# Mixture-of-experts stage: scatter woven with the next gather behind the whole down product, and a weight ring of one slab more

## The chip, the cores and the metric

One core of one Trainium2 chip. The time is the device time of one execution in microseconds (us), and of several executions the median counts. Matmuls run on TensorE (PE; its weight loads are listed as PEld), elementwise work on VectorE (DVE), ScalarE (ACT) and GpSimd (POOL). SyncE (SP) issues the transfers from memory in one queue, in its program's order; sixteen DMA engines carry them out.

## The reference, cut to what matters

One layer over 512 tokens of 1024 channels, all in float32. A token mixer (a state-space branch and a Fourier branch) fills the first part of the kernel and isn't touched. The second part is a routed feed-forward layer with 16 experts, where each expert picks its 64 best tokens:

```
aff = softmax(h @ w_router);  top_aff, top_idx = top_k(aff.T, 64)
xe  = h[top_idx]                                   # gather, 16 experts x 64 tokens
hid = silu(xe @ w_e_gate) * (xe @ w_e_up)          # 1024 -> 1024 each
ye  = (hid @ w_e_down) * top_aff                   # 1024 -> 1024
out = zeros.at[top_idx].add(ye)                    # scatter
x   = x + g2 * rms_norm(out, w)
```

The weights of the experts are 16 x 3 x 4 MB, about 201 MB, each byte read once.

## The kernel before, in words

The experts run two at a time, in eight pairs (the loop `for q in range(NE // 2)`, L1116). The two experts of a pair have 64 tokens each and take the two column halves of the TensorE array, so that their matmuls run side by side. Per pair:

- DVE compares the tokens' slot numbers with a row of counters (L1121), which gives a 0/1 matrix `pm_` of 512 tokens by 128 slots.
- The gather multiplies `h2` with `pm_` (L1129): eight channel tiles `kt`, four token chunks each. ACT moves each tile into `xe` and applies the modulation (L1131). After every two tiles the gate product `pg` uses them (`expert_mm`, L1082, with `ks=(k,)`), so gather and gate product alternate in four rounds.
- `pm_` is transposed into `pT` (L1135), and each slot's affinity `afs` is computed (L1139). Then comes the up product `pu` (L1082 again).
- ACT applies silu (L1150), DVE multiplies by `pu` (L1151), TensorE transposes `hid` (L1154), and ACT moves the transposes out (L1155).
- The down product `pd` (L1167) runs in four column blocks `m` of 256. After each block `scatter` (L1089) forms a high part `yeh` on ACT (L1093) and the rest `yel` on DVE (L1094), multiplies both with `pT` (L1100, eight matmuls of 256 columns) and adds them to the accumulators `acc` on DVE (L1105). In the last pair it also squares the sums (L1111, L1113) and multiplies them by the gate row on POOL (L1114).

At the end comes the norm (L1173 to L1175) and the output (L1183, L1184).

The weights come as slabs of 1 MB (128 partitions x 2048 floats): eight each for gate, up and down per pair, 24 in all, two (one per expert) for each quarter `k` of a product. `ring_tile` (L1051) places slab after slab in slots of on-chip memory, first in the order of `FIRST`, then round `RING` (15 slots). A slab's transfer is issued when TensorE has read the slot's earlier content for the last time; SP issues in the slabs' order and waits at the first that isn't free. The first 19 entries of `FIRST` are different slots.

```python
    FIRST = (21, 22, 23, 8, 10, 11, 12, 13, 14, 16, 0, 3, 9, 4, 6, 5, 1, 2, 20, 21, 22, 8, 23)
    RING = (10, 11, 12, 13, 14, 16, 0, 3, 4, 1, 2, 20, 21, 22, 23)
```

Slots 7 and 8 hold `xe` and `pm_` of alternating pairs, slot 9 holds `hid` and its transposes, slots 5 and 6 `acc`. On-chip result banks (PSUM) come from two pools: five for products (`MM`), three for small things (`SD`: gather, transposes, scatter).

The order of instructions on each engine is set by the framework's scheduler, from the order in which they are traced and from its own estimate of when inputs are ready; it may move an instruction past others. `in_order` pins the traced order where it is called; in the expert stage it isn't.

Of the kernel before, what the change touches and what calls it, by code (L numbers as in the profile page):

```python
# [9 lines left out]
F32 = mybir.dt.float32  # L10
# [21 lines left out]
# columns of the per-partition constants  # L32
# [26 lines left out]
def block_kernel(ctx: ExitStack, tc: tile.TileContext, a: dict, out: bass.AP):  # L59
# [62 lines left out]
    # ---------------------------------------------------------------- x, norms  # L122
# [24 lines left out]
    # triangular and other masks  # L147
# [17 lines left out]
    # sel[32 g + i, i] = 1: sums the partial products of the column tiles  # L165
# [5 lines left out]
    # the table of Silu, which has the functions of the first steps too  # L171
# [11 lines left out]
    def rstd_tok(y, ssum, m, t, n):  # L183
        """y = 1/sqrt(ssum/n + eps)"""
# [30 lines left out]
    def bcast_rows(dst, src, n):  # L215
        """dst[:, 128 c + t] = src[t, c] on all partitions"""
# [7 lines left out]
    def sum_squares(pss, src, slots, w):  # L224
        """sums over the channels, token-major"""
# [40 lines left out]
    def warm(dst, n):  # L266
        """keeps the tensor engine's clock up over a wait"""
# [62 lines left out]
    # ---------------------------------------------------------------- in-projection  # L330
# [5 lines left out]
    def conv(psum, ct, dst, rows, width):  # L336
        """centred depthwise convolution of a channel tile, then SiLU"""
# [14 lines left out]
    def wtile(idx, slot=None):  # L352
        """hi and lo parts of unit idx of the streamed weights"""
# [18 lines left out]
    # first group: contraction tiles in the outer loop, as their modulation becomes known  # L372
# [41 lines left out]
    # dt of both directions, token-major: chunks 0..3 of x, then 0..1 of ctx  # L414
# [6 lines left out]
    # the products with the hi and with the lo part on partitions 0.. and 48.., added up when they are transposed  # L421
# [7 lines left out]
    with tc.high_priority():  # L429
# [6 lines left out]
        # softplus(raw + bias) = max(v, 0) + 2 atanh(u / (2 + u)), u = exp(-|v|)  # L436
# [49 lines left out]
        # context: weights of the final states, [chunk, (dir, head)]  # L486
# [11 lines left out]
        # running sums as rows, through memory, to be read back on all partitions  # L498
# [7 lines left out]
    # ---------------------------------------------------------------- bidirectional SSD of a group  # L506
# [4 lines left out]
    def ssd(g):  # L511
# [40 lines left out]
        # C.B of every chunk, [s, t]  # L552
# [6 lines left out]
        # skip term  # L559
# [79 lines left out]
    # remaining modulation rows: products with silu(c) along the free dimension  # L639
# [14 lines left out]
    # the recurrences interleaved with the projections that they leave the tensor engine to  # L654
# [10 lines left out]
    def weave(pattern, main, fill):  # L665
        """steps of both in the pattern's order, then what is left of them"""
# [12 lines left out]
    # ---------------------------------------------------------------- Fourier branch  # L679
# [43 lines left out]
    # ---------------------------------------------------------------- merge of the branches  # L723
# [37 lines left out]
    # router with the second norm's gain folded in, and the logits of its shift  # L761
# [36 lines left out]
    def mix_step(dst, w, c, kt):  # L798
        """adds the contribution of contraction tile kt to one half of the output projection of a token chunk"""
# [6 lines left out]
    # the order of the units in the stream: 12 of w_ssd_out with one of the first half of w_out after every third  # L806
# [33 lines left out]
    # ---------------------------------------------------------------- output projection, residual, second norm  # L840
# [5 lines left out]
    # affinities, the chunks c as [c % 2, c / 2]  # L846
# [5 lines left out]
    # sums of squares over the channels: [step, (mixer output of the step's chunk, residual of the chunk before), half]  # L852
# [5 lines left out]
    def half(c, n, p):  # L858
        """mean square and product with the gate row, for one half of the columns"""
# [9 lines left out]
    def rsqrt(step, lo, hi, between=()):  # L869
        """rsd = 1/sqrt(mean square + eps) of the step's columns lo..hi"""  # L870
# [29 lines left out]
    def logits(c):  # L900
        """by expert, the contraction over four column tiles; then summed and token-major"""
# [36 lines left out]
    # affinities by expert: those of the first half of the tokens on partitions 0.., of the second on 32..  # L938
# [65 lines left out]
    # ---------------------------------------------------------------- routing: top CAP tokens of every expert  # L1004
# [4 lines left out]
    # the CAP-th of both sorted halves together: i of one and CAP - i of the other  # L1009
# [5 lines left out]
    # on all partitions; tokens above it, and those equal to it in order, fill the slots  # L1015
# [10 lines left out]
    # running counts of both kinds; every token above the value comes before those equal to it  # L1026
# [16 lines left out]
    # ---------------------------------------------------------------- experts, two at a time  # L1043
    acc = None
    wnames = ("w_eg", "w_eu", "w_ed")

    FIRST = (21, 22, 23, 8, 10, 11, 12, 13, 14, 16, 0, 3, 9, 4, 6, 5, 1, 2, 20, 21, 22, 8, 23)
    RING = (10, 11, 12, 13, 14, 16, 0, 3, 4, 1, 2, 20, 21, 22, 23)
# [7 lines left out]
    def weights(kind, q):  # L1056
        """slabs of the two experts, alternating"""
        tiles = {}
        for k in range(4):
            if kind == "w_eu" and q == NE // 2 - 1 and k == 2:  # L1060
                G3.append(ring_tile("g3")[:, 0:1024])
                for n in range(2):
                    p = SD(f"g3{n}")
                    bcast_rows(p, mod2[:, 24 + 4 * n:28 + 4 * n], 4)
                    act.copy(G3[0][:, 512 * n:512 * n + 512], p)
            for e in range(2):
                tiles[k, e] = ring_tile(f"{kind}{q}{k}{e}")
            cuts = CUTS[k] if kind == "w_ed" and q == NE // 2 - 1 else (0, 2048)
# [5 lines left out]
    G3 = []  # L1074

    def expert_mm(w, lhs, pout, ks=(0, 1, 2, 3)):
        for k in ks:
            for i in range(2):
                kt = 2 * k + i
                for n in range(2):  # L1080
                    for e in range(2):
                        pe.matmul(pout[n][64 * e:64 * e + 64, :], lhsT=lhs(kt)[:, 64 * e:64 * e + 64],  # L1082
                                  rhs=w[k, e][:, 1024 * i + 512 * n:1024 * i + 512 * n + 512],
                                  start=(kt == 0), stop=(kt == KT - 1))
# [4 lines left out]
    def scatter(q, m, pd, pT, afs):  # L1089
        """adds the experts' outputs in a block of 256 columns to their tokens; after the last pair their squares and gate"""  # L1090
        yeh = tp.tile([P, 256], F32, name=f"yeh{q}{m}", tag="sz")
        yel = tp.tile([P, 256], F32, name=f"yel{q}{m}", tag="xw")
        act.activation(R(yeh), pd, AF.Copy, scale=afs)  # L1093
        dve.scalar_tensor_tensor(R(yel), pd, afs, yeh, op0=ALU.mult, op1=ALU.subtract)  # L1094
        for i in range(2):
            p = SD(f"sc{q}{m}{i}")
            pv = v(p, 0, 2, 256)
            for c in range(2):
                for k, y in enumerate((yeh, yel)):
                    pe.matmul(pv[:, c], lhsT=R(pT[:, 2 * i + c]), rhs=R(y), start=(k == 0), stop=(k == 1))  # L1100
            av = v(acc[i], 0, 2, 1024)[:, :, 256 * m:256 * m + 256]
            if q == 0:
                dve.tensor_copy(av, pv)
            else:
                dve.tensor_add(av, av, pv)  # L1105
            if q == NE // 2 - 1:
                for c in range(2):
# [8 lines left out]
    for q in range(NE // 2):  # L1116
# [17 lines left out]
        for c in range(NCH):  # L1134
            pe.transpose(p[:, 128 * c:128 * c + 128], pm_[:, c], ident)  # L1135
# [130 lines left out]
```

## Time and profile before

| | |
|---|---|
| runs, median (lowest to highest) | 1171.88 us (1169.7 to 1176.0), 3 runs |
| profiled execution, span of its instructions | 1169.3 us (no other time of it is given) |
| TensorE busy | 1118.4 us, 96% of the span |
| DVE, ACT, POOL busy | 45%, 37%, 8% |
| memory traffic | 289.70 MB, 248 GB/s over the span |
| gate, up, down products: busy | 126.6, 118.1, 120.9 us |
| gather, scatter products: busy | 67.7, 34.1 + 31.1 us |

Busy time of TensorE is a union of matmuls whose ends are modelled, so how densely they run is read from the distance of their starts, not from this share. The expert stage runs from about 651 us to the end; `PEclk` is the granted clock of TensorE, 1.00 for 2.4 GHz and 0.50 for 1.2 GHz.

### The profile page before, as it was taken

How to read it: one execution, taken by the hardware profiler on the slowest of the kernel's cores; microseconds unless marked ns; L12 is line 12 of the kernel's file. 1: busy time of each engine (PE TensorE's matmuls, PEld its weight loads, DVE VectorE, ACT ScalarE, POOL GpSimd, SP SyncE). 2: the span in 40 equal slices, each digit the busy share in tenths (PEclk: the TensorE clock that was granted, in tenths of full speed). 3: DMA queues.
4: the chain of work that ended last, by engine and by line, in shares of the span. 5: the costliest groups of instructions: out<-in, count | busy, mean ns of one | idle time of the engine just before them, and what ended most of it. 6: DMA issues, size and time to landing. Idle time of an engine off the chain costs nothing. (4 is left out here: it accounts for less than half of the span.)

```text
span 1169.3 us, 16246 instructions
## 1 busy us (share of the span) xinstructions
PE 1118.4 (96%) x6596; PEld 766.3 (66%) x6596; DVE 529.0 (45%) x917; ACT 431.3 (37%) x688; POOL 96.7 (8%) x118
## 2 busy tenths in 40 slices
PE   8999999999899999999999999999999999999994
PEld 4788868778688887887886545454545454554542
DVE  5677988686686668744346211111102030201115
ACT  4357886877774532423236111111111111110112
POOL 1002132211121100001011000000000000000004
PEclk9999999999999999999999999999999999999997
DMA  8613243322424388733386698999999999999951
GB/s 313 232 44 94 89 111 89 111 76 88 135 84 153 151 301 303 257 121 100 103 338 263 244 363 323 392 419 420 417 384 420 374 419 372 420 370 420 358 170 73
DMA packets 57019, 289.70 MB, mean 248 GB/s; under 512 B 6928, under 2 KB 15600, under 8 KB 29936
## 3 DMA queue, kind: packets, MB, share of 16 engines
q1 hardware_dynamic: 56944, 288.66, 65.3%
q8 instruction: 52, 0.85, 0.3%
q14 instruction: 23, 0.19, 0.0%
HBM read 286.43 MB, written 2.21 MB: 247 GB/s over the span
## 5 line engine op out<-in xcount | busy, mean ns | idle before, releaser
L1151 DVE TENSOR_TENSOR hid<-hid,pu 128x512 f32<-128x512 f32 x16 | 11.0, 688 | 297.2 <-PE pu L1082 297.2
L1082 PE MATMUL pg<-w_eg,pk 128*64 128x512 f32 x512 | 126.6, 599 | 0.0
L1167 PE MATMUL pd<-w_ed,hid 128*64 128x256 f32 x1024 | 120.9, 382 | 0.0
L1082 PE MATMUL pu<-w_eu,pk 128*64 128x512 f32 x512 | 118.1, 593 | 0.0
L272 ACT CAST whl<-raw 128x1024 fp32r<-128x1024 f32 x71 | 74.4, 1050 | 113.4 <-PE gt L334 41.0
L273 DVE TENSOR_TENSOR whl<-raw,whl 128x1024 fp32r<-128x1024 f32 x71 | 90.6, 1279 | 46.0 <-ACT whl L272 45.7
L1167 PEld LDWEIGHTS pd<-w_ed,hid 128*64 128x64 f32 x1024 | 72.8, 137 | 38.2 <-ACT hid L1155 1.2
L1082 PEld LDWEIGHTS pu<-w_eu,pk 128*64 128x64 f32 x512 | 42.7, 136 | 66.5 <-issue 65.8
L1131 ACT ACTIVATE pk<-xe,mod 128x128 f32<-128x128 f32 x64 | 29.3, 457 | 140.4 <-PE xe L1129 140.4
L1082 PEld LDWEIGHTS pg<-w_eg,pk 128*64 128x64 f32 x512 | 36.6, 136 | 61.0 <-issue 56.9
L1129 PEld LDWEIGHTS xe<-pk,h 128*128 128x128 f32 x512 | 60.7, 191 | 21.3 <-issue 20.1
L1129 PE MATMUL xe<-pk,h 128*128 128x128 f32 x512 | 67.7, 281 | 0.2 <-DVE pk L1121 0.2
L1093 ACT ACTIVATE yeh<-pd,afs 128x256 fp32r<-128x256 f32 x32 | 15.1, 473 | 136.4 <-PE pd L1167 136.4
L1094 DVE SCALAR_TENSOR_TENSOR yel<-pd,afs,yeh 128x256 fp32r<-128x256 f32 x32 | 15.5, 484 | 105.1 <-ACT yeh L1093 105.1
L1114 POOL TENSOR_TENSOR acc<-acc,g 128x512 f32<-128x512 f32 x8 | 10.3, 1302 | 516.3 <-ACT jk L1113 515.9
L334 PE MATMUL gt<-hhi,whl 128*128 128x512 f32 x128 | 50.2, 392 | 0.0
L332 PE MATMUL gt<-hhi,whl 128*128 128x512 f32 x128 | 50.0, 391 | 0.0
L333 PE MATMUL gt<-hlo,whl 128*128 128x512 f32 x128 | 49.8, 389 | 0.0
L573 DVE TENSOR_TENSOR rm<-rm,misc 128x768 f32<-128x768 f32 x32 | 31.8, 995 | 39.0 <-POOL rm L571 38.9
L332 PE MATMUL pj<-hhi,whl 128*128 128x512 f32 x120 | 48.5, 404 | 0.0
L334 PE MATMUL pj<-hhi,whl 128*128 128x512 f32 x120 | 48.2, 401 | 0.0
L333 PE MATMUL pj<-hlo,whl 128*128 128x512 f32 x120 | 48.0, 400 | 0.0
(408 smaller groups left out, 2352.0 us busy)
## 6 DMA issues: line engine op xcount, KB each, us to landing
w_eg<-in_w_eg_dram SPq DMA_DIRECT2D x64, 1024.0 KB, 9.8
w_eu<-in_w_eu_dram SPq DMA_DIRECT2D x64, 1024.0 KB, 10.9
w_ed<-in_w_ed_dram SPq DMA_DIRECT2D x56, 1024.0 KB, 7.7
raw<-in_w_rest_dram SPq DMA_DIRECT2D x71, 512.0 KB, 3.4
wm<-in_wmod_dram SPq DMA_DIRECT2D x16, 1024.0 KB, 6.8
rm<-rowd SPq DMA_DIRECT2D x32, 384.0 KB, 5.6
wmod<-in_wmod_dram SPq DMA_DIRECT2D x8, 1024.0 KB, 7.8
w_ed<-in_w_ed_dram SPq DMA_DIRECT2D x12, 512.0 KB, 6.7
```

The source lines that it names most:

```text
L272: act.copy(hi, src)
L273: dve.tensor_sub(lo, src, hi.bitcast(F32))
L332: pe.matmul(dst, lhsT=wh, rhs=hi, start=(kt == 0 and start), stop=False)
L333: pe.matmul(dst, lhsT=wh, rhs=lo, start=False, stop=False)
L334: pe.matmul(dst, lhsT=wl, rhs=hi, start=False, stop=(kt == nk - 1 and stop))
L573: dve.tensor_tensor(mk, mk, csm[:, :, c, hs:hs + 3][:, :, :, None].to_broadcast([P, 2, 3, 128]), op=ALU.add)
L1082: pe.matmul(pout[n][64 * e:64 * e + 64, :], lhsT=lhs(kt)[:, 64 * e:64 * e + 64], rhs=w[k, e][:, 1024 * i + 512 * n:1024 * i + 512 * n + 51 ...
L1093: act.activation(R(yeh), pd, AF.Copy, scale=afs)
L1094: dve.scalar_tensor_tensor(R(yel), pd, afs, yeh, op0=ALU.mult, op1=ALU.subtract)
L1129: pe.matmul(p[:, 0:128], lhsT=tv(h2, c)[:, 128 * kt:128 * kt + 128], rhs=pm_[:, c], start=(c == 0), stop=(c == NCH - 1))
L1131: act.activation(xe[:, kt], p[:, 0:128], AF.Identity, bias=SH2[:, kt:kt + 1], scale=G2[:, kt:kt + 1])
L1167: pe.matmul(pd[-1][64 * e:64 * e + 64, o:o + 256], lhsT=hidT[:, kt, 64 * e:64 * e + 64], rhs=wd[m, e][:, 256 * kt:256 * kt + 256], start=( ...
```

## The change

Everything ahead of the experts stays (comments there are dropped). In the expert stage:

- `gather(q)` is a function of its own that yields after each of its eight channel tiles. Four tiles share one small bank and are moved out together. Pair 0's gather runs whole before the loop; the gather of pair `q + 1` runs at the end of pair `q`, tile by tile in turn with the eight steps of `scatter(q)` (two column halves of 512 by four token chunks, two matmuls of 512 columns each).
- The gate product is one run of 64 matmul instructions without gathers between, as the up product was. The affinities, the transposes of `hid` and those of `pm_` follow the up product in this order.
- The down product of all four blocks runs ahead of the scatter. `scaled` writes high and low parts of 512 columns into slot 8 (`ys`). Only in the last pair they are formed per block of 256, and block `m - 1` is scattered behind block `m` of the product (`scatter_last`).
- `xe` and `pm_` use slot 7 alone; `hid`, its transposes and `pT` move to small buffers. `RING` gets slot 9 and has 16 slots. The last pair's gate row `G3` is made between its gate and up products.
- `hold_order` pins the traced order of the whole stage on TensorE, and on no other engine.

```diff
+    FIRST = (21, 22, 23, 8, 10, 11, 12, 13, 14, 16, 0, 3, 9, 4, 6, 5, 1, 2, 20, 21, 22, 23, 10, 11)
+    RING = (12, 13, 14, 16, 0, 3, 9, 4, 1, 2, 20, 21, 22, 23, 10, 11)
...
+    def gather(q):
+        pk_ = S(f"pk{q}", 7)
+        xe, pm_ = v(pk_, 0, 8, 128), v(pk_, 1024, 4, 128)
+        dve.tensor_tensor(pm_.rearrange("p c (e s) -> p c e s", e=2), iota[:, None, None, :].to_broadcast([P, 4, 2, 64]),
+                          slot[:, :, 2 * q:2 * q + 2][:, :, :, None].to_broadcast([P, 4, 2, 64]), op=ALU.is_equal)
+        picked[q] = (xe, pm_)
+        for kt in range(KT):
+            if kt % 4 == 0:
+                p = v(SD(f"xe{q}{kt}"), 0, 4, 128)
+            for c in range(NCH):
+                pe.matmul(p[:, kt % 4], lhsT=tv(h2, c)[:, 128 * kt:128 * kt + 128], rhs=pm_[:, c], start=(c == 0),
+                          stop=(c == NCH - 1))
+            if kt % 4 == 3:
+                for k in range(kt - 3, kt + 1):
+                    act.activation(xe[:, k], p[:, k % 4], AF.Identity, bias=SH2[:, k:k + 1], scale=G2[:, k:k + 1])
+            yield
+
+    def scatter(q, ys, pT):
+        for n in range(2):
+            for c in range(NCH):
+                p = SD(f"sc{q}{n}{c}")
+                for k in range(2):
+                    o = 1024 * k + 512 * n
+                    pe.matmul(p, lhsT=R(pT[c // 2][:, 128 * (c % 2):128 * (c % 2) + 128]), rhs=R(ys[:, o:o + 512]),
+                              start=(k == 0), stop=(k == 1))
+                av = tv(acc, c)[:, 512 * n:512 * n + 512]
+                if q == 0:
+                    dve.tensor_copy(av, p)
+                else:
+                    dve.tensor_add(av, av, p)
+                yield
...
+    def scaled(ys, lo, hi, pd, afs):
+        yh_, yl_ = ys[:, lo:hi], ys[:, 1024 + lo:1024 + hi]
+        act.activation(R(yh_), pd, AF.Copy, scale=afs)
+        dve.scalar_tensor_tensor(R(yl_), pd, afs, yh_, op0=ALU.mult, op1=ALU.subtract)
...
+    run(gather(0))
+    for q in range(NP):
+        last = q == NP - 1
+        xe, pm_ = picked.pop(q)
+        wg = weights("w_eg", q)
+        expert_mm(wg, xe, pg)
...
+        expert_mm(wu, xe, pu)
...
+            if last:
+                scaled(ys, 256 * m, 256 * m + 256, pd[:, o:o + 256], afs)
+                if m > 0:
+                    scatter_last(m - 1, ys, pT)
+            elif m % 2 == 1:
+                scaled(ys, 256 * m - 256, 256 * m + 256, pd, afs)
+        if last:
+            scatter_last(3, ys, pT)
+        else:
+            weave("fsfsfsfsfsfsfsfs", scatter(q, ys, pT), gather(q + 1))
+    hold_order(begin_experts, {pe.engine})
```

In `weave`, `f` takes a step of the gather and `s` a step of the scatter.

## Rows read from the trace of the kernel before

**Rows 1.** Busy time of the engines in stretches of one pair; columns in the first line.

```profile
core 0: us, PE busy (x) PEld busy (x) DVE busy (x) ACT busy (x) POOL busy (x), PEclk, DMA share, GB/s
653.38:713.81 60.43, 58.94 (x374) 31.71 (x373) 9.68 (x16) 9.98 (x20) 0.00 (x0) 1.00 0.84 329
962.96:1026.36 63.40, 61.08 (x374) 33.26 (x376) 9.05 (x15) 8.81 (x19) 0.00 (x0) 1.00 0.97 398
```

**Rows 2.** Chain that ended last, one pair: start us, us, engine, output, count.

```profile
966.54 1.98 PE xe L1129 x16
...
981.52 0.59 PE pT L1135 x4
982.11 0.80 PE as L1139 x8
...
986.48 13.75 PE pu L1082 x61
1000.33 0.70 DVE hid L1151
1001.07 0.65 PE ht L1154 x4
1001.72 3.65 PE pd L1167 x32
1006.51 0.98 PE sc L1100 x6
1007.49 3.65 PE pd L1167 x32
```

**Rows 3.** Waits of the transfer queue from 640 us on: total us, times, longest.

```profile
SPq L1071 <- PE pg L1082: 185.8, 37, 19.2
SPq L1071 <- PE pd L1167: 133.5, 28, 8.1
```

**Rows 4.** Line L1071 (weight transfers) from 1117 to 1124 us, the last of them.

```profile
L1071 SPq DMA_DIRECT2D w_ed<-in_w_ed_dram x8: 328/426/665, 1119.0 to 1122.4; - x8
...
DMA to landing us min/median/max: 4.5/7.5/7.9
```

**Rows 5.** Engines in two stretches with transfers always queued, columns as in rows 1.

```profile
747.00:779.00 32.00, 30.43 (x222) 18.76 (x219) 9.06 (x15) 3.98 (x8) 0.00 (x0) 1.00 1.01 420
742.00:858.00 116.00, 112.03 (x714) 61.81 (x712) 18.11 (x30) 16.38 (x36) 0.00 (x0) 1.00 1.01 416
```

**Rows 6.** Transfers issued from 300 to 651 us: count, size, median us to landing.

```profile
w_eg<-in_w_eg_dram SPq DMA_DIRECT2D x8, 1024.0 KB, 6.9
w_eu<-in_w_eu_dram SPq DMA_DIRECT2D x8, 1024.0 KB, 9.9
w_ed<-in_w_ed_dram SPq DMA_DIRECT2D x3, 1024.0 KB, 12.0
```

**Rows 7.** DVE in order of time, after a pair's up product.

```profile
1000.93 0.69 DVE L1121 TENSOR_TENSOR pk<-mats,slot 128x512 f32<-128x512 f32 x1
```

**Rows 8.** Groups of one pair, 962.96 to 1026.36 us: busy us, mean ns, idle before.

```profile
L1105 DVE TENSOR_TENSOR acc<-acc,sc 128x512 f32<-128x512 f32 x8 | 5.1, 684 | 3.0 <-PE sc L1100 3.0
L1131 ACT ACTIVATE pk<-xe,mod 128x128 f32<-128x128 f32 x8 | 3.7, 457 | 16.8 <-PE xe L1129 16.8
L1094 DVE SCALAR_TENSOR_TENSOR yel<-pd,afs,yeh 128x256 fp32r<-128x256 f32 x4 | 1.9, 484 | 14.0 <-ACT yeh L1093 14.0
```

**Rows 9.** TensorE in order of time: first gather of the stage.

```profile
651.42 2.02 PE L1129 MATMUL xe<-pk,h 128*128 128x128 f32 x16 [0.17 <-DVE pk L1121]
```

**Rows 10.** ACT and POOL in order of time, after the last down product.

```profile
1151.31 0.47 ACT L1093 ACTIVATE yeh<-pd,afs 128x256 fp32r<-128x256 f32 x1 [1.10 <-PE pd L1167]
...
1156.69 1.26 POOL L1114 TENSOR_TENSOR acc<-acc,g 128x512 f32<-128x512 f32 x1 [0.37 <-DVE jk L1111]
```

**Rows 11.** TensorE in order of time: a wait ahead of a lower clock.

```profile
631.21 0.40 PE L912 MATMUL lg<-sel,lp 128*128 128x16 f32 x2 [1.69 <-ACT lp L911]
```

**Rows 12.** Engines in the stretch after that wait, columns as in rows 1.

```profile
631.90:635.20 3.30, 2.92 (x21) 1.68 (x12) 2.52 (x8) 1.39 (x4) 0.00 (x0) 0.50 1.02 432
```

More of the change, by code (lines that the diff above doesn't have):

```diff
@@ L100, in in_order, with hold_order @@
             if i.engine in engines:
+                if i.engine in last:
+                    tc.add_manual_dep(i, last[i.engine].name,
+                                      mybir.DependencyInfo(mybir.DependencyClass.NoSync, mybir.DependencyReason.DATA),
+                                      reason="order")
+                last[i.engine] = i
+    def hold_order(begin, engines_):
+        last = {}
+        for i in nc.cur_bb.bb.instructions[begin:]:
+            if i.engine in engines_:
                 if i.engine in last:
@@ L1059, in weights @@
         for k in range(4):
[L1060 to L1065, printed above, removed]
             for e in range(2):
                 tiles[k, e] = ring_tile(f"{kind}{q}{k}{e}")
-            cuts = CUTS[k] if kind == "w_ed" and q == NE // 2 - 1 else (0, 2048)
+            cuts = CUTS[k] if kind == "w_ed" and q == NP - 1 else (0, 2048)
             for lo, hi in zip(cuts, cuts[1:]):
@@ L1072, in weights @@
         return tiles
[L1074 to L1084, printed above, removed]
@@ L1116, in block_kernel, with expert_mm @@
-    for q in range(NE // 2):
-        pk_ = S(f"pk{q}", 7 + q % 2)
-        xe = v(pk_, 0, 8, 128)
-        pm_ = v(pk_, 1024, 4, 128)
-        pT = tp.tile([P, 4, 128], F32, name=f"pTs{q}", tag="cb")
+    def expert_mm(w, xe, pout):
+        for kt in range(KT):
+            for n in range(2):
+                for e in range(2):
+                    o = 1024 * (kt % 2) + 512 * n
+                    pe.matmul(pout[n][64 * e:64 * e + 64, :], lhsT=xe[:, kt, 64 * e:64 * e + 64],
+                              rhs=w[kt // 2, e][:, o:o + 512], start=(kt == 0), stop=(kt == KT - 1))
@@ new lines, in scatter @@
+    def scatter(q, ys, pT):
+        for n in range(2):
+            for c in range(NCH):
[10 more added lines that the diff above has]
+                yield
@@ new lines, in scatter_last @@
+    def scatter_last(m, ys, pT):
+        for i in range(2):
+            p = v(SD(f"sl{m}{i}"), 0, 2, 256)
+            for c in range(2):
+                for k in range(2):
+                    o = 1024 * k + 256 * m
+                    pe.matmul(p[:, c], lhsT=R(pT[i][:, 128 * c:128 * c + 128]), rhs=R(ys[:, o:o + 256]), start=(k == 0),
+                              stop=(k == 1))
+            av = v(acc[i], 0, 2, 1024)[:, :, 256 * m:256 * m + 256]
+            dve.tensor_add(av, av, p)
+            for c in range(2):
+                junk = tp.tile([P, 256], F32, name=f"jk{m}{i}{c}", tag="sz")
+                sq = fst[:, m, 2 * i + c:2 * i + c + 1]
+                if m == 3 and i == 1:
+                    dve.scalar_tensor_tensor(junk, av[:, c], 1.0 / D, av[:, c], op0=ALU.mult, op1=ALU.mult, accum_out=sq)
+                else:
+                    act.activation(junk, av[:, c], AF.Square, scale=D ** -0.5, accum_out=sq)
+            pool.tensor_tensor(av, av, G3[:, None, 256 * m:256 * m + 256].to_broadcast([P, 2, 256]), op=ALU.mult)
@@ L1133, in block_kernel @@
-        p = SD(f"pT{q}")
-        for c in range(NCH):
-            pe.transpose(p[:, 128 * c:128 * c + 128], pm_[:, c], ident)
-        act.copy(R(pT), v(p, 0, 4, 128))
+        expert_mm(wg, xe, pg)
+        hid = [tp.tile([P, 512], F32, name=f"hid{q}{n}", tag="sz") for n in range(2)]
+        for n in range(2):
+            act.activation(hid[n], pg[n], AF.Silu)
+        wu = weights("w_eu", q)
+        if last:
+            G3 = ring_tile("g3")[:, 0:1024]
+            for n in range(2):
+                p = SD(f"g3{n}")
+                bcast_rows(p, mod2[:, 24 + 4 * n:28 + 4 * n], 4)
+                act.copy(G3[:, 512 * n:512 * n + 512], p)
@@ L1137, in block_kernel @@
+        pu = [MM(f"pu{q}{n}") for n in range(2)]
+        expert_mm(wu, xe, pu)
+        for n in range(2):
+            dve.tensor_mul(hid[n], hid[n], pu[n])
         p = SD(f"as{q}")
@@ L1142, in block_kernel @@
             act.copy(afs[64 * e:64 * e + 64], p[64 * e:64 * e + 64, 2 * q + e:2 * q + e + 1])
-        wu = weights("w_eu", q)
-        pu = [MM(f"pu{q}{n}") for n in range(2)]
-        expert_mm(wu, lambda kt: xe[:, kt], pu)
-        hh = S(f"hid{q}", 9)
-        hid, hidT = hh[:, 0:1024], v(hh, 1024, 8, 128)
+        hidT = []
         for n in range(2):
-            hv = hid[:, 512 * n:512 * n + 512]
-            act.activation(hv, pg[n], AF.Silu)
-            dve.tensor_mul(hv, hv, pu[n])
             p = SD(f"ht{q}{n}")
@@ L1153, in block_kernel @@
             for k in range(4):
-                pe.transpose(p[:, 128 * k:128 * k + 128], hv[:, 128 * k:128 * k + 128], ident)
-            act.copy(hidT[:, 4 * n:4 * n + 4], v(p, 0, 4, 128))
+                pe.transpose(p[:, 128 * k:128 * k + 128], hid[n][:, 128 * k:128 * k + 128], ident)
+            hidT.append(v(tp.tile([P, 512], F32, name=f"hidT{q}{n}", tag="cb"), 0, 4, 128))
+            act.copy(hidT[n], v(p, 0, 4, 128))
+        p = SD(f"pT{q}")
+        for c in range(NCH):
+            pe.transpose(p[:, 128 * c:128 * c + 128], pm_[:, c], ident)
@@ L1156, in block_kernel @@
+        pT = [tp.tile([P, 256], F32, name=f"pTs{q}{i}", tag="xw") for i in range(2)]
+        for i in range(2):
+            act.copy(R(pT[i]), p[:, 256 * i:256 * i + 256])
         wd = weights("w_ed", q)
[L1157 removed]
         if q == 0:
             acc = [S("acc0", 6), S("acc1", 5)]
[L1160 to L1169 removed]
+        ys = S(f"ys{q}", 8)
@@ new lines, in block_kernel @@
+        for m in range(4):
+            o = 256 * (m % 2)
+            if m % 2 == 0 or last:
+                pd = MM(f"pd{q}{m}")
+            for kt in range(KT):
+                for e in range(2):
+                    pe.matmul(pd[64 * e:64 * e + 64, o:o + 256], lhsT=hidT[kt // 4][:, kt % 4, 64 * e:64 * e + 64],
+                              rhs=wd[m, e][:, 256 * kt:256 * kt + 256], start=(kt == 0), stop=(kt == KT - 1))
+            if last:
[4 more added lines that the diff above has]
+                scaled(ys, 256 * m - 256, 256 * m + 256, pd, afs)
```

55 lines of the change are left out of this document (7 added, 48 removed).

## The prediction

> **What bounds the kernel now.** I read the stretches by pair first. A late pair takes 63.40 us, an early one 60.43 [rows 1]; the starts of the eight gate products give 60.4, 60.5, 61.9 and four times 63.4. That the late period repeats to 0.01 us says that one engine's program sets it. The chain of waits says which: a pair is TensorE from end to end, with one DVE link after the up product [rows 2]. The reader should look at how the links follow. The up product, which runs alone, needs 13.75 us for its 64 instructions. A block of the down product needs 3.65, but the next one starts 5.77 later (1001.72 to 1007.49): 0.98 is scatter, and 1.14 is TensorE waiting for ACT's high part and filling again. Four such blocks are 4.6 us of waiting per pair.
>
> Then the transfers. They are nearly always running in a late pair (share 0.97), but at 398 GB/s, where stretches with a full queue show 420, and 416 over a long one [rows 1, 5]. The difference is the queue waiting for TensorE to free slots: 185.8 us for gate products, 133.5 for down products [rows 3]. No wait of TensorE in the late pairs ends with a transfer. The last pieces are issued at 1122.4 us and land at most 7.9 us later, by 1130.3 [rows 4], 21 us before the last down product ends at 1151.2 (ACT reads it at 1151.3 [rows 10]). So TensorE is the bound, and the transfers follow it with some 20 us in hand. But they are no distant second: 24 slabs of 1.0486 MB at 416 GB/s (2.521 us each) are 60.5 us per pair, at 420 GB/s (2.497) 59.9. A TensorE that becomes faster than that hits the transfers.
>
> **TensorE's pair after the change**, each item from rows 2:
> - Three products of equal column count, each in one run: 3 x 13.75 = 41.25. For the down product the row of one block (3.65, four times: 14.6) is the upper bound, since each of those ends in a drain that a run has once; 13.75 is the nearest row of a whole run.
> - Between up and down: affinities 0.80, transposes of `hid` 2 x 0.65, of `pm_` 0.59, together 2.7. The affinities cover DVE's first multiplication (0.70), and the transposes of `pm_` cover ACT's move of `hid`. Bounds: 2.0 if they overlap as the short rows do, 3.4 if DVE's second multiplication shows.
> - Gather, 64 instructions at 1.98 per 16: 7.92. Scatter, the same columns as 4 x 0.98: 3.92.
> - The wait for the high part, 4.6 per pair, goes: the down product is followed by a gather step, and the first scatter step needs a half that was scaled two blocks earlier. The second half is needed half a weave (5.9 us) after the product; scaling it takes ACT and DVE about 0.5 + 0.5 per 256 columns, 2 us for 512 [rows 8, 10]. What could be late next is the comparison that builds the next `pm_`: now it must wait until the slot's old content is read, which ends with the transposes of `pm_`. The trace has DVE making it as soon as it may, at 1000.93, in the middle of the pair [rows 7], and DVE's order isn't pinned; so I cost it at nothing. If DVE kept the traced order, TensorE would stand for scaling and comparison, about 2.2 us per pair.
>
> Sum: 41.25 + 2.7 + 7.92 + 3.92 = 55.8 us, against 63.4. Moved evictions are covered too: ACT's four gather moves (4 x 0.457) have a scatter step and the first half of the gate product beside them, DVE's additions (0.68) the next gather step [rows 8].
>
> **The transfers after it.** 55.8 is below 60.5, so the pace is soon the transfers', and the sum must follow them.
> - 19 slabs are issued before the stage begins [rows 6], as now; the first 19 slots are the same. The 20th needs the first quarter of pair 0's gate product. That now comes behind the whole gather: 651.42 [rows 9] + 7.92 + 3.44 = 662.8, and 4.8 us to land (the shortest landings are 4.5 [rows 4]): 667.6. Here the change loses some 6 us: that quarter used to come behind two of the eight tiles (1.98), not all (7.92).
> - 21 slabs then land without a pause, to 718. The 41st needs the first quarter of pair 1's gate product: 651.4 + 7.9 + 55.8 + 3.4 = 718.6; it lands at 723.3.
> - From there slots come free faster than slabs arrive: pair 2's first quarter ends at 774.4, its slot's next slab is due at 783.8, and the margin grows by 4.7 us per pair. 151 more slabs at 2.521 us (the long stretch, which has its small interruptions in it): 380.7, so the last lands at 1104.0. At 420 GB/s 1100.4; with another 1 us lost per pair, 1110.
> - TensorE alone would end its last product at 659.3 + 8 x 55.8 - 11.84 + 2.2 (the gate row) = 1096, 8 us earlier. So it waits for weights in the last three or four pairs, and 1.3 us more per pair would still cost nothing.
> - After the last landing a last quarter block remains, 0.9 us and its drain: 1105.2.
> - The end after the product took 1169.3 - 1151.2 = 18.1 us. Block 2 is now scattered behind the product of block 3, and POOL has its two gate multiplications (1.26 each [rows 10]) still to do when those of block 3 come; the norm's chain shares DVE with them. Bounds 0 and 2.5, I take 1.2.
>
> Span: 1105.2 + 18.1 + 1.2 = 1124.5, against 1169.3. The median of the runs shown is 2.6 above this span; the forecast for the median is **1127 us**, with 1118 to 1133 as its own range (420 GB/s and no longer end; 1 us lost per pair).
>
> A rule speaks against this. TensorE will wait about 1.6 us for every two slabs in the starved blocks (5.04 us of arrival, 3.44 of work), and here the one fall of the granted clock in mid-kernel, to 0.50 (1.2 GHz), came right after TensorE had stood 1.69 us for ACT [rows 11, 12]. The Trainium skill, page "TensorE: Matmul & The Clock Gate", section "Loop structure matters more than you think", names a transfer awaited between matmuls as the loop that goes cold, and the fall in this trace agrees. It is the second rival.
>
> **Rivals.**
> 1. The transfers keep their old pace. Against one slot more stand 319 us of waiting for slots [rows 3]; if landings stay as they are, to 1130.3, the end is 1130.3 + 1.2 + 19.3 + 2.6 = 1153. Against it: those waits are for TensorE's products, which now end sooner. Chance 0.08.
> 2. The clock falls in starved blocks. Such a block takes 6.9 us instead of 3.44. With three per pair a pair is 66 us, which also lets the transfers get ahead, so that the next one isn't starved: in the mean (66 + 60.5) / 2, 2.8 us more in each of four pairs, 1138. Chance 0.12.
> 3. TensorE's run isn't dense (comparison in traced order, small banks, drains between weave steps): above 1.3 us per pair each further one costs 7. At 58 to 60 per pair, 1133 to 1147. Chance 0.12.
> 4. Slower: the weave runs in series. The gather holds one of three small banks for four steps, and each scatter step holds one until DVE has added it. If every scatter step has to wait for the DVE addition before it, with a hand-over each way (0.68 + 0.4), eight of these are 8.7 us per pair; with the comparison's 2.2 in front, 66.7, and TensorE ends the last product at 659.3 + 7 x 66.7 + 46.2 = 1172 rather than 1151.2: about 1194. It decides from 63.5 us per pair on. Against it: a gather step (0.99) lies between any two scatter steps. Chance 0.05.
>
> **How the numbers follow.** My forecast has 0.60, and 0.03 stays for what I don't name. The range 1118 to 1147 takes in the forecast, the second rival and the third. About 0.5% (6 us) is what a measurement of this kernel can tell from no change: faster by more holds for all but the fourth rival and parts of the third and of the unnamed: 0.89; within it 0.04; slower 0.07.
>
> **What would show it.** Right: late pairs of about 60.5 us with the transfers at 414 to 420 GB/s; waits of TensorE that end with weight transfers, in the last pairs only; no wait for the high part ahead of the scatter; gate products in runs of 13.75; the last weights landing about 1104, 1 to 2 us before the last product ends. Wrong: early pairs (1 to 3) of more than 57 us, which would be rival 3 or 4; a clock below 1.00 in the last pairs (2); a queue that still waits for slots in the last pairs (1).

## The result and the profile after

The changed kernel took 1128.32 us (median of four runs, 1126.16 to 1131.0) against 1172.34 before: a ratio of 0.9625, with a 95% interval from 0.9598 to 0.9652. The forecast was 1127, its own range 1118 to 1133. The profiled execution spans 1125.0 us, forecast 1124.5.

The page's slices first (40 equal parts of the span). From the 27th slice to the 38th the transfers run at 418 to 421 GB/s; in the kernel before, whose line comes first, every second slice from the 30th to the 38th dips to 358 to 384:

```profile
GB/s 313 232 44 94 89 111 89 111 76 88 135 84 153 151 301 303 257 121 100 103 338 263 244 363 323 392 419 420 417 384 420 374 419 372 420 370 420 358 170 73
```

```profile
PEclk8999999999999999999999999999999999999997
DMA  7622252332514368853337849999999999999993
GB/s 302 237 73 68 77 142 65 99 99 86 166 42 131 132 240 320 293 198 111 116 112 313 331 177 420 389 419 419 418 419 420 419 420 419 419 419 421 418 406 125
```

Stretches of the changed kernel: an early pair (pair 1), one pair's length (60.00 us) later on, and the starved part of pair 6, in which TensorE waits for weights; columns as in [rows 1]:

```profile
713.10:768.27 55.17, 55.17 (x357) 30.54 (x356) 9.07 (x13) 7.51 (x19) 0.00 (x0) 1.00 0.98 403
943.00:1003.00 60.00, 57.38 (x360) 30.78 (x358) 9.07 (x13) 7.52 (x18) 0.00 (x0) 1.00 1.01 419
1027.00:1045.00 18.00, 15.37 (x133) 9.32 (x131) 1.44 (x2) 1.93 (x5) 0.00 (x0) 1.00 1.02 420
```

The early pair (63.40 for a late one before [rows 1]) has TensorE busy in all of its 55.17 us. The later stretch has 419 GB/s and idle time on TensorE. In the starved part TensorE is idle for 2.6 of 18 us, and its clock stays at 1.00. Over the whole stage, TensorE's waits that end with a transfer are these (total us, times, longest), all in pairs 4 to 6:

```profile
PE pd L1202 <- DMA w_ed<-in_w_ed_dram: 7.0, 6, 1.3
```

The chain through an early pair answers to [rows 2]; columns are start us, us, engine, output, count:

```profile
768.34 13.88 PE pg L1083 x64
782.23 13.73 PE pu L1083 x64
795.96 0.99 PE as L1175 x8
796.96 0.92 PE ht L1183 x8
797.88 0.44 PE pT L1188 x4
798.31 13.96 PE pd L1202 x128
812.28 1.09 PE xe L1100 x8
813.36 0.47 PE sc L1114 x2
813.83 0.89 PE xe L1100 x8
814.72 0.46 PE sc L1114 x2
...
818.77 0.68 PE sc L1114 x2
```

Three products of 13.7 to 14.0 us each, 2.35 us between the second and the third, and then steps of 0.89 (gather, the first 1.09) and 0.47 (scatter) in turn. One scatter step of the eight takes 0.68; together the eight take 3.93 us, and the gather takes 7.32. From 860.25 on, in the down product of pair 3, the chain is another one. It runs through transfers:

```profile
860.25 19.91 DMA w_eg<-in_w_eg_dram
880.22 21.39 DMA w_eu<-in_w_eu_dram
901.67 19.88 DMA w_ed<-in_w_ed_dram
```

It goes on like that to 1041.34. The waits of the transfer queue from 640 us on (total, times, longest) answer to [rows 3]:

```profile
SPq L1075 <- DMA w_eg<-in_w_eg_dram: 92.9, 46, 2.1
SPq L1075 <- DMA w_ed<-in_w_ed_dram: 88.9, 50, 2.1
SPq L1075 <- DMA w_eu<-in_w_eu_dram: 81.2, 38, 3.6
SPq L1075 <- PE pg L1083: 79.6, 15, 24.6
SPq L1075 <- PE pd L1202: 23.3, 8, 8.5
```

The queue now waits mostly for transfers, 263 us in all, and 103 us for gate and down products, where it had been 319. Of these 103 us, 77 lie ahead of 770 us, in the first two pairs, and 17 more ahead of 785. The queue's own order of time shows the six `w_ed` issues of the start, with a pause from 636.63 to 661.60 us among them, and the 41st slab's issue at 716.78:

```profile
636.63 32.65 SPq L1075 DMA_DIRECT2D w_ed<-in_w_ed_dram  x6
...
716.78 11.10 SPq L1075 DMA_DIRECT2D w_ed<-in_w_ed_dram  x8
```

Four views of the end. TensorE in pair 6, between blocks of the down product, waits for weights; the last transfer is issued at 1098.1 and lands 5.3 us later, at 1103.4 (before: 1130.3 [rows 4]); POOL has four gate multiplications in a row behind the last product; and in pair 7, from its gate product to the end of its last down product, TensorE is busy in 49.11 of 49.25 us, so that it waits for weights no more:

```profile
1036.35 3.67 PE L1202 MATMUL pd<-w_ed,hidT 128*64 128x256 f32 x32 [1.31 <-DMA w_ed<-in_w_ed_dram]
1041.34 3.67 PE L1202 MATMUL pd<-w_ed,hidT 128*64 128x256 f32 x30 [1.32 <-DMA w_ed<-in_w_ed_dram]
```

```profile
L1075 SPq DMA_DIRECT2D w_ed<-in_w_ed_dram x9: 327/328/328, 1087.9 to 1098.1; - x9
...
DMA to landing us min/median/max: 5.3/7.7/10.2
```

```profile
1104.74 1.28 POOL L1141 TENSOR_TENSOR acc<-acc,g 128x512 f32<-128x512 f32 x1
1108.27 5.36 POOL L1141 TENSOR_TENSOR acc<-acc,g 128x512 f32<-128x512 f32 x4 [2.24 <-ACT jk L1140]
```

```profile
1056.25:1105.50 49.25, 49.11 (x310) 24.14 (x309) 6.45 (x11) 10.21 (x33) 4.50 (x4) 1.00 0.92 367
```

### The profile page after: what moved, and what is told of

Its sections match the earlier page's. It is cut to its first block, busy times and chain, and to the rows that moved or that the text cites. A ratio compares the mean times of both kernels' runs of the same rounds, so it can differ in the third digit from the quotient of the medians.

```text
span 1125.0 us, 16049 instructions
## 1 busy us (share of the span) xinstructions
PE 1082.2 (96%) x6484; PEld 750.5 (67%) x6484; DVE 529.8 (47%) x903; ACT 421.8 (37%) x682; POOL 96.6 (9%) x118
## 5 line engine op out<-in xcount | busy, mean ns | idle before, releaser
L1202 PE MATMUL pd<-w_ed,hidT 128*64 128x256 f32 x1024 | 115.6, 381 | 7.2 <-DMA w_ed<-in_w_ed_dram 7.0
L1083 PE MATMUL pu<-w_eu,pk 128*64 128x512 f32 x512 | 113.8, 593 | 0.0
L284 DVE TENSOR_TENSOR whl<-raw,whl 128x1024 fp32r<-128x1024 f32 x71 | 91.0, 1284 | 46.2 <-ACT whl L283 45.8
L1083 PE MATMUL pg<-w_eg,pk 128*64 128x512 f32 x512 | 111.6, 594 | 0.0
L1202 PEld LDWEIGHTS pd<-w_ed,hidT 128*64 128x64 f32 x1024 | 72.7, 137 | 47.2 <-DMA w_ed<-in_w_ed_dram 10.6
L1083 PEld LDWEIGHTS pu<-w_eu,pk 128*64 128x64 f32 x512 | 37.2, 137 | 74.6 <-issue 70.0
L1100 PEld LDWEIGHTS xe<-pk,h 128*128 128x128 f32 x512 | 65.3, 191 | 7.4 <-issue 3.3
L1147 DVE SCALAR_TENSOR_TENSOR ys<-pd,afs,ys 128x512 fp32r<-128x512 f32 (+1 forms) x18 | 12.4, 692 | 116.0 <-ACT ys L1146 116.0
L1104 ACT ACTIVATE pk<-xe,mod 128x128 f32<-128x128 f32 x64 | 24.1, 457 | 72.8 <-PE xe L1100 72.8
L1146 ACT ACTIVATE ys<-pd,afs 128x512 fp32r<-128x512 f32 (+1 forms) x18 | 11.5, 640 | 105.9 <-PE pd L1202 64.0
## 6 DMA issues: line engine op xcount, KB each, us to landing
w_eg<-in_w_eg_dram SPq DMA_DIRECT2D x64, 1024.0 KB, 19.9
w_eu<-in_w_eu_dram SPq DMA_DIRECT2D x64, 1024.0 KB, 19.9
```

Source lines behind the costliest of these rows:

```text
L284: dve.tensor_sub(lo, src, hi.bitcast(F32))
L1083: pe.matmul(pout[n][64 * e:64 * e + 64, :], lhsT=xe[:, kt, 64 * e:64 * e + 64], rhs=w[kt // 2, e][:, o:o + 512], start=(kt == 0), stop=(kt ...
L1100: pe.matmul(p[:, kt % 4], lhsT=tv(h2, c)[:, 128 * kt:128 * kt + 128], rhs=pm_[:, c], start=(c == 0), stop=(c == NCH - 1))
L1104: act.activation(xe[:, k], p[:, k % 4], AF.Identity, bias=SH2[:, k:k + 1], scale=G2[:, k:k + 1])
L1146: act.activation(R(yh_), pd, AF.Copy, scale=afs)
L1147: dve.scalar_tensor_tensor(R(yl_), pd, afs, yh_, op0=ALU.mult, op1=ALU.subtract)
```

## The experiments

The theory to be tested: TensorE's pair fell from 63.4 to 55.2 us, and from pair 4 on the transfers hold the pace. The rivals: TensorE still sets the pace throughout; the ring's extra slab or the weave itself carries the gain. What comes before the stage takes a different time from run to run (the first gather starts between 649 and 656 us in the profiles), so the table gives each profile's stage from its first gather on. A pair is counted from one gate product's start to the next.

| kernel | median us | pairs 0 to 6, us | last product ends | last weights | stage |
|---|---|---|---|---|---|
| before | 1172.3 | 60.4, 60.5, 61.8, 63.4 x 4 | 499.8 | 478.9 | 517.9 |
| changed | 1128.3 | 55.2 x 4, 57.8, 59.9, 59.9 | 454.9 | 452.8 | 474.3 |
| changed, no down loads | 1116.9 | 55.2 x 7 | 442.5 | | 462.0 |
| before, no down loads | 1158.0 | 60.7, 62.5, 60.5 x 5 | 486.0 | | 503.8 |
| scatter per block | 1150.9 | 60.4 x 7 | 479.1 | 462.9 | 498.5 |
| ring of 15 | 1128.9 | 55.2 x 4, 60.2, 60.0, 59.9 | 457.1 | 455.2 | 476.5 |
| scatter, then gather | 1130.7 | 56.4 x 5, 58.6, 59.9 | 456.9 | 453.8 | 476.3 |
| scatter in up product | 1134.7 | 51.3, 57.8 x 6 | 460.4 | 450.0 | 479.8 |
| the same, tail | 1132.8 | 51.3, 57.8 x 6 | 461.7 | 450.5 | 479.8 |
| tail alone | 1125.9 | 55.2 x 4, 57.8, 60.0, 59.9 | 456.0 | 452.7 | 474.1 |
| head and tail | 1125.9 | 57.7, 59.9, 55.2 x 3, 57.7, 60.4 | 453.4 | 448.9 | 471.5 |
| order not pinned | 1154.9 | 55.2, 55.2, 59.7, 61.8 x 4 | 482.8 | 460.6 | 500.4 |

**A third of the transfers taken away, after and before.** In both kernels the down product reads slabs that are there already, and the down weights are never loaded. First the changed kernel:

```diff
-        wd = weights("w_ed", q)
+        wd = wu
```

> The changed kernel, but the down product reads the up product's slabs again, and the down weights are never loaded (a third of the weight traffic is left out; the sums come out different). Theory (from pair 4 on the transfers set the pace, before that TensorE): pairs stay at 55.2 us to the end, no wait of TensorE ends with a transfer, the last gate product begins at 1044 rather than 1056, and the time falls by about 12 us, to 1116. Rival (TensorE sets the pace throughout, and its late pairs of 60 us are long for another reason, such as a slower weave): no change, 1128.

Measured: 1116.87 us, ratio to before 0.9524 (0.95 to 0.9547). A late pair:

```profile
937.08:992.26 55.18, 55.18 (x358) 30.55 (x357) 9.07 (x13) 7.52 (x20) 0.00 (x0) 1.00 0.75 305
```

The reader should see 55.18 busy of 55.18 where the changed kernel's late pairs have idle time and 59.9: the transfers were worth 12 us, and without them TensorE runs as in the early pairs. In the kernel before, pair 0 uses the gate slabs and the ring steps over the eight slots:

```diff
-        wd = weights("w_ed", q)
+        wd = wu if q else wg
+        ring[0] += 8
```

> The kernel before, with the down product reading the up product's slabs (in pair 0 the gate product's) and the down weights never loaded (a third of the weight traffic is left out; the sums come out different). The scheduler may choose another order on TensorE, as in the early pairs (60.4 us) or the late ones (63.4). Theory (TensorE was the bound, with weights in hand): no pair under 60 us, the time between 1150 and 1172. Rival (the transfers were a second bound that the old kernel touched too): pairs of 56 us or less, under 1135.

Measured: 1158.0 us, 0.9877 (0.9857 to 0.9897), with a late pair at

```profile
899.47:959.93 60.46, 58.92 (x374) 31.72 (x373) 9.05 (x15) 8.77 (x19) 0.00 (x0) 1.00 0.73 277
```

No pair is under 60 us although the transfers run at 277 GB/s. So TensorE was the bound before. The 3 us per late pair that were gained (63.4 to 60.5) come with another order on TensorE, which the scheduler chose: in this late pair the gate product is four whole quarters and the up product one run of 13.95 us, as in pair 1 of the kernel before, while a late pair of the kernel before mixes the end of the gate product with the up product. All pairs but the second (62.5) have about the length of the early ones.

**The scatter put back behind each block.** `scatter_block` is the old scatter on the parts in `ys`; the next gather then runs by itself behind the fourth block:

```diff
-            elif m % 2 == 1:
-                scaled(ys, 256 * m - 256, 256 * m + 256, pd, afs)
+            else:
+                scaled(ys, 256 * m, 256 * m + 256, pd[:, o:o + 256], afs)
+                scatter_block(q, m, ys, pT)
...
-            weave("fsfsfsfsfsfsfsfs", scatter(q, ys, pT), gather(q + 1))
+            run(gather(q + 1))
```

> The changed kernel with one part undone: each block of 256 columns of the down product is scaled and scattered at once, in every pair, and the next gather runs after the four, unwoven. Ring, runs of the gate product and pinned order stay. Theory: TensorE waits about 1.1 us per block for the high part again, 4.6 us per pair, pairs are about 59.8 us from the first on, the last product ends at 1125 instead of 1105.5, the time is 1148. Rival (the waits are hidden by the transfers, what counts is the ring or the dense gate product): 1128 to 1131.

Measured: 1150.9 us, 0.9826 (0.9792 to 0.9859). TensorE in order of time:

```profile
814.97 3.67 PE L1216 MATMUL pd<-w_ed,hidT 128*64 128x256 f32 x32
819.24 1.61 PE L1129 MATMUL sb<-ys,pTs 128*128 128x256 f32 x8 [0.60 <-ACT ys L1160]
820.78 3.67 PE L1216 MATMUL pd<-w_ed,hidT 128*64 128x256 f32 x32
```

TensorE's waits for ACT ahead of the scatter in the whole stage (total us, times, longest):

```profile
PE sb L1129 <- ACT ys L1160: 17.2, 28, 0.7
```

Again 0.6 us of idle time ahead of each scatter, blocks 5.81 us apart, and pairs of 60.4: undoing this one part costs 5.3 us per pair and 24 us of stage. All of it lies in the blocks: four are 23.2 us, where down product and scatter take 13.96 + 3.93 = 17.9 in the change. But only 17.2 / 7 = 2.5 us of it per pair is idle time; the rest is a longer scatter (1.54 us from its start to the next block, where a quarter of 3.93 is 0.98) and blocks of 3.67 instead of a quarter of 13.96. TensorE is then slower than the transfers from the first pair on, and nothing covers it. This kernel keeps the pinned order, the gate product in one run and the ring, and its pairs are as long as the early ones before: against the late pairs before, these parts are worth 3.0 us per pair, and the scatter behind the whole product, with its weave, the other 5.3.

**The ring of 15.**

```diff
-    RING = (12, 13, 14, 16, 0, 3, 9, 4, 1, 2, 20, 21, 22, 23, 10, 11)
+    RING = (12, 13, 14, 16, 0, 3, 4, 1, 2, 20, 21, 22, 23, 10, 11)
```

> The changed kernel with slot 9 used once and then left out of the ring, so 15 slots as before. Theory: the slab counts for little, since a landing every 2.5 us and at most eight transfers under way need few free slots; the 40th slab waits for the next pair's first gate quarter, one slab earlier than with 16, which costs one landing, 2.5 us: 1130.8, and pairs 5 and 6 stay at 60. Rival (the extra slab carries the gain): 1140 or more, with the transfer queue waiting for TensorE in the late pairs.

Measured: 1128.93 us, 0.9634 (0.9615 to 0.9653), against 0.9625 for the change: not told apart by timing, and far from the rival's 1140. In the traces the 41st slab lands 73.4 us into the stage instead of 70.9, and every later landing is 2.4 us later: one landing, as expected.

**The weave undone.**

```diff
-            weave("fsfsfsfsfsfsfsfs", scatter(q, ys, pT), gather(q + 1))
+            weave("ssssssssffffffff", scatter(q, ys, pT), gather(q + 1))
```

> The changed kernel with the weave undone: the eight scatter steps first, the eight gather steps behind them, all else the same. Each scatter step then waits for DVE's addition (0.68 us against 0.45 of matmuls) through the three small banks, and the first gather moves are late: about 2 us more per pair for TensorE, 57 instead of 55.2. Theory (slack against the transfers, about 12 us over the stage): early pairs 57, late pairs still 60, the end at most 2 us later, 1128 to 1130. Rival (the weave itself carries the gain): 7 x 2 = 14 us or more, 1142.

Measured: 1130.68 us, 0.9639 (0.9615 to 0.9662). The same set had the changed kernel again,

> The changed kernel as it is, for the other three of this set: 1128.

and that took 1127.81 us, 0.9617 (0.9592 to 0.9642). TensorE's pair is 1.26 us longer, 56.43 for 55.17, less than the 2 us expected. Over seven pairs that is 8.8 us, and the stage grew by 2.0: the rest went into the wait for weights. So the turn-by-turn weave by itself carries little of the gain; what counts is that the scatter stands behind the whole down product.

**The scatter moved into the next up product.** The runs so far point to a version that frees slots sooner: without the scatter in front of it, the next gate product starts earlier.

```diff
-            weave("fsfsfsfsfsfsfsfs", scatter(q, ys, pT), gather(q + 1))
+            run(gather(q + 1))
+            late = scatter(q, ys, pT)
...
         for kt in range(KT):
+            if fill is not None:
+                next(fill, None)
...
-        expert_mm(wu, xe, pu)
+        expert_mm(wu, xe, pu, late)
```

> The changed kernel with the scatter moved on: the gather of pair q + 1 runs alone behind the down product, and the scatter of pair q is woven with the up product of pair q + 1 (a step ahead of each contraction tile). The sum of TensorE's work is the same. Theory: the transfers set the end, and their last loss is that the 41st slab has to wait for the first gate quarter of pair 1; without the scatter in front this comes 3.8 us sooner, and so do later releases; every landing from there on moves up by 1 to 3 us and the end with it: 1125 to 1127. Rival (only TensorE's total counts): 1128. If the late gathers' evictions stall the gate product: over 1130.

Measured: 1134.67 us, 0.9685 (0.966 to 0.971): slower than the change, a miss. The half of the theory on transfers held, the 41st slab is issued 62.3 us into the stage instead of 66.2 and lands 1.4 us sooner. The gate product doesn't stall behind the gather alone: in this trace it takes 13.95 us, as in the change, so the third outcome named ahead of the run isn't the reason. What failed is "the sum of TensorE's work is the same":

```profile
784.13 0.73 PE L1116 MATMUL sc<-ys,pTs 128*128 128x512 f32 x2
784.79 1.94 PE L1085 MATMUL pu<-w_eu,pk 128*64 128x512 f32 x8
786.66 0.73 PE L1116 MATMUL sc<-ys,pTs 128*128 128x512 f32 x2
```

The steps are 2.53 us apart, where eight up instructions in a run (13.73 / 8 = 1.72) and a scatter step (0.47) are 2.19. Each of eight steps loses 0.34, 2.6 us per pair as the pairs show, and at 57.8 TensorE is the bound to the end. The weave with the gather loses nothing of the kind (0.89 and 0.47 make 1.36, and the steps are 1.36 apart). By the tiles in the rows, the gather uses the whole array (`128*128`), as the scatter does, and the up product column halves (`128*64`); that the loss comes from this difference is inferred, not tested. With the tail edit that is shown next:

> As the run before, and in the last pair the scatter of block m - 1 stands ahead of the sixth contraction tile of block m of the down product instead of behind the whole block, so that the additions, squares and gate products of block 2 run beside the last matmuls. Theory: the end behind the last product shrinks from 19.5 us to about 18, another 1 to 1.5 us: 1124 to 1125.5.

Measured: 1132.8 us, 0.9658 (0.9638 to 0.9677), a miss too. The end behind the last product is 18.1 us, as expected, but that product ends 1.3 us later, and the stage is 479.8 us in both.

**Tail, then head and tail.**

```diff
             for kt in range(KT):
+                if last and m > 0 and kt == 5:
+                    scatter_last(m - 1, ys, pT)
...
-                if m > 0:
-                    scatter_last(m - 1, ys, pT)
```

> The changed kernel; in the last pair alone the scatter of block m - 1 stands ahead of the sixth contraction tile of block m. Theory: 19.5 us from the last down product to the end become 18, the time 1126.5.

Measured: 1125.86 us, 0.959 (0.9574 to 0.9606); the changed kernel in the same set:

> The changed kernel as it is, beside the other three kernels of this set, as in the second set: 1128.

1128.58 us, 0.9613 (0.959 to 0.9637). The intervals overlap, and the traces say that the edit did little: from the last product to the end 18.1 us instead of 19.4, but that product ends 1.1 us later, since the scatter of block 2 now stands in front of its last matmuls. The stage is 0.2 us shorter. That the median is 2.7 us lower can't be put down to it. The second kernel has the head too:

```diff
-    run(gather(0))
+    g0 = gather_first()
+    next(g0)
...
+        if q == 0:
+            next(g0)
+            for k in range(4):
+                expert_mm(wg, xe, pg, (2 * k, 2 * k + 1))
+                next(g0, None)
+                next(g0, None)
...
+        if q == 1:
+            acc += [S("acc0", 6), S("acc1", 5)]
+            run(late)
...
+        elif q == 0:
+            run(gather(1))
+            late = scatter(0, ys, pT)
```

> The last run's edit, and the head of the stage: pair 0's gather is spread over its gate product again, two tiles ahead of each quarter; pair 0's scatter runs in one piece behind pair 1's gate product, so that the accumulators' two slots hold two of pair 1's gate slabs first. TensorE loses about 2 us in the first two pairs, which it has in hand. Theory: the transfers resume about 5 us sooner, the 41st slab has no wait, the last weights land 3 to 4 us sooner, the time is 1122 to 1124. Rival (the first quarters then free slots only every 5.6 us, and the gain stays there): 1126.

Measured: 1125.94 us, 0.9594 (0.9575 to 0.9613). In the trace the last weights land 448.9 us into the stage instead of 452.7 with the tail alone, the 3 to 4 us that were expected, and the stage is 471.5, 2.6 us less. But the time was to be 1122 to 1124, and 1125.94 is the rival's 1126: a miss by the time, though the transfers moved as the theory says. The timed runs don't tell this kernel from the tail alone; its profiled stage also began 3.4 us later (at 652.7 for 649.2). Both are ahead of the kernel before by more than 4%; that one of them is ahead of the change stays open at this size.

**The order not pinned.**

```diff
-    hold_order(begin_experts, {pe.engine})
```

> The changed kernel without the pinned order; the scheduler then puts some gather matmuls between the two column halves of down products, and reorders up products. Theory: matmuls of the two halves that no longer stand side by side lose their overlap (0.43 us for two of 512 columns); early pairs take 56 to 60 us, late ones stay at 60 by the transfers: 1128 to 1140. Rival (the pinned order alone carries the gain): 1160 or more.

Measured: 1154.91 us, 0.9832 (0.9813 to 0.985), a miss: far nearer to the rival than to the theory. TensorE in a late pair:

```profile
929.76 0.65 PE L1202 MATMUL pd<-w_ed,hidT 128*64 128x256 f32 x2
930.62 2.27 PE L1100 MATMUL xe<-pk,h 128*128 128x128 f32 x18 [0.21 <-DVE pk L1093]
932.82 3.67 PE L1202 MATMUL pd<-w_ed,hidT 128*64 128x256 f32 x32
936.43 1.83 PE L1100 MATMUL xe<-pk,h 128*128 128x128 f32 x14
938.18 3.67 PE L1202 MATMUL pd<-w_ed,hidT 128*64 128x256 f32 x32
942.68 1.74 PE L1114 MATMUL sc<-ys,pTs 128*128 128x512 f32 x6 [0.82 <-ACT ys L1146]
944.74 0.73 PE L1114 MATMUL sc<-ys,pTs 128*128 128x512 f32 x2 [0.32 <-DVE acc L1120]
```

The scheduler has broken up the down product: the gather stands between its blocks, and the scatter waits for ACT in the middle of it. It also puts `pg` and `pu` one by one in turn. Pairs 0 and 1 have the changed kernel's length, the late ones 61.8. So the pinned order is worth 26 of the 43.5 us of stage, and without it the same code keeps 17.5. That the scheduler moves work forward where it expects weights to be late is inferred: it reorders only later pairs here, and with fewer transfers the kernel before had no late order. The other half wasn't tested: no run pins the kernel before and changes nothing else.

## Why the prediction was right, point by point

- **TensorE the bound, transfers some 20 us in hand**: shown. Without a third of the transfers the kernel before has no pair under 60 us, and the table has its last weights 20.9 us ahead of the last product's end.
- **Pair of 55.8**: 55.17. The products were 13.7 to 14.0 for 13.75, the part between 2.35 for 2.7; the gather 7.32 for 7.92 and the scatter 3.93 for 3.92. The five add up to the pair. The comparison was made early, as costed; TensorE waited for it once, in pair 0, for 0.2 us.
- **The wait for the high part goes**: shown by undoing it, 5.3 us per pair for the 4.6 counted. But what goes is less than half waiting. The scatter piece in [rows 2] has six of the eight matmuls (x6), so that the 1.14 us called waiting hold the first two; TensorE's idle time ahead of the four scatters of that pair is 0.66, 0.18, 0.62 and 0.60 us, 2.1 in all. The scatter's 3.92 was counted from the same six of eight, where the eight take 1.43 us per block (1005.99 to 1007.42); that it fits the new scatter to 0.01 us is luck.
- **First landing 667.6, 41st slab 723.3, last 1104.0**: 666.3, 721.5 and 1103.4. The 151 intervals after the 41st took 381.9 us, 2.529 each for 2.521. Counted from the stage's first gather, the 41st was 1.0 us early (70.9 for 71.9) and the intervals 1.2 us longer in all, so two small errors cancel.
- **Starved in the last three or four pairs**: pairs 4, 5 and 6, 57.8 to 59.9 us, with waits of 1.3 us at most where 1.6 was counted. Pair 7 wasn't starved: its last product ended 2.2 us behind the last landing, where 1.2 was counted, and TensorE's own work set that end. Pair 7 took 49.25 us from its gate product on, for the 46.2 of the sum, which leaves out the two scatters of 1.15 us each between its last three blocks.
- **Last product 1105.2, then 19.3 us**: 1105.6 and 19.4. The first of these is near by luck in part, since the last landing, from which it was reckoned, didn't set it.
- **The range's lower end, 1118**: it doesn't follow from the two items named for it. 420 GB/s takes off 3.6 us and an end that grows by nothing 1.2, which makes 1122. The measured 1128.3 lies above both.

Against the rivals: the old pace of the transfers is refuted by the queue's waits. The clock did not fall in the starved blocks: TensorE waited up to 1.31 us at a time between runs of 3.67 us of matmuls, and the granted clock was 1.00 (2.4 GHz) in the starved part of pair 6, with the page's clock slices at 9 from the second to the last but one. The Trainium skill ("TensorE: Matmul & The Clock Gate", section "Loop structure matters more than you think") speaks of a long wait for a transfer between every matmul; the waits here were short ones between 32 matmuls, so no run here shows its case. Nor does a wait like that of [rows 11], which was for ACT and not for a transfer, by itself bring the fall: at the same place the changed kernel's TensorE stands 1.70 us for ACT, and the clock behind it is 1.00, where it had been 0.50 [rows 12]:

```profile
630.95 0.40 PE L923 MATMUL lg<-sel,lp 128*128 128x16 f32 x2 [1.70 <-ACT lp L922]
```

```profile
631.60:634.90 3.30, 2.29 (x24) 1.26 (x17) 2.98 (x9) 1.53 (x5) 0.00 (x0) 1.00 1.01 425
```

TensorE's run was dense. The weave did not run in series.

One thing the prediction didn't price: it took TensorE's dense run from the way the new code is written and gave the pinned order no term of its own. Taking the pin away costs 26 us of stage, putting the scatter back per block 24. The two together are more than the gain of 43.5, so they overlap: the order is worth about as much as the scatter's new place, which it holds. By the early pairs of the kernel before (60.4 for 63.4), pinning alone would have brought some 13 us there (four late pairs of 3.0 and 1.4 in pair 2); that is an estimate, not a run.

## What to carry to other kernels

Where one engine is the bound and another has slack, price both per round before counting a gain: here 8.2 us per pair were won, but only 3.5 of them in pairs that the transfers hold at 59.9. The 43.5 us of stage are made up like this: the last weights land 26.1 us sooner; the 20.9 us that they had been ahead of the last product's end shrink to 2.2, which is another 18.7; and the end behind that product grew by 1.3. A scheduler that orders by its own estimate can undo a good order, here for 26 us; pin the order of the engine that is the bound. And what to weave with matters: scatter steps lost next to nothing beside gather steps, and 0.34 us each between steps of the up product.

## What the runs showed of the hardware that I had not expected

At most eight weight transfers were under way at a time, before and after. Once slots were plentiful, each issue came when the eighth transfer before it had landed, and a slab took 19.9 us from issue to landing, eight times 2.49. Here it cost nothing that the traces show: with eight the transfers ran at 419 to 420 GB/s. It may be why the sixteenth slot of the ring is worth so little; no run varies the eight, and whether the program or the chip sets it isn't shown. The view of the transfer issues from 940 to 1000 us:

```profile
L1075 SPq DMA_DIRECT2D w_ed<-in_w_ed_dram x8: 327/327/328, 944.1 to 961.5; - x8
...
DMA to landing us min/median/max: 19.6/19.9/19.9
```
